# Two-layer encoder on one core: the second output product takes all its rows into the seven block products, and attention is drawn ahead

## The chip, the cores and the metric

The kernel runs on one core of one Trainium2 chip. The metric is device microseconds of one execution: the median before is 959.88 us of three runs (959.16 to 960.65).

## The reference

Two layers over 512 tokens of width 1024, in float32. What matters here is the second one (i = 1): eight query heads over two key/value heads, four memory heads, a gate, one output projection and the residual.

```python
for i in range(DEPTH):
    h = rmsnorm(x, norm_g[i])
    ...
    proj = jnp.einsum('bsd,de->bse', h, w_in_b[j])     # q | k | v | q_mem | gate
    o_mix = mixer_axial_gqa(...)                       # 8 heads of 128, rms norm, rotary, softmax
    ...
    o_mem = memory_attention(q_mem, mem_h, w_mem_kv[i], mem_qn_g[i], mem_kn_g[i])   # 4 heads
    y = jnp.concatenate([o_mix, o_mem], axis=-1) * jax.nn.silu(gate)                # 512 x 1536
    x = x + jnp.einsum('bse,ed->bsd', y, w_out[i])                                  # 1536 x 1024
```

## The kernel before

**Block products.** A 512-token projection is done by `s_chunk` (L376): the activations and the weights are cut into 2 x 2 blocks, and seven products of sums of blocks replace eight block products. The list `PRODUCTS` names the form of the activations that each takes: 12, 11, S1, S2, S4, S3, 22. S1 = A21 - A22, S2 = S1 - A11, S4 = A12 + S2, S3 = A11 - A21. Each product accumulates in PSUM banks (`pj`); at its end `keep` copies a bank to SBUF (ScalarE, a tile `sn`, L384) or `add` adds it to a kept one (VectorE, L401), and `diff` (L395) makes one difference of two kept tiles. What comes out goes to an evacuation `ev`.

**Precision.** Every float32 operand is split in a high part in the matmul's format and a low part, so each product is three matmuls: high by high (L172), low by high or high by low (L173), and the third (L176). For the weights the high part `wh` is a cast on ScalarE (L307) and the low part `wo` a subtraction on VectorE (L317), each for a 128 x 1024 tile. A *unit* is what one such tile feeds: in the output product 12 matmuls of 512 columns, in a gate 24 of 256.

**Weights.** `Weights` loads tiles on SyncE's queue, makes the sums T1 to T4 that the block products need by accumulating DMAs on GpSimd's queue, and casts two units ahead. `PLAN` lists the chunks in order, and for each kind how many tiles it has. The second layer's last entries are "W2b" (the block part of the output product, two units for each of the seven products) and twice "O1" (the rest).

**Order.** All engines' instructions are written in one program. A `Driver` counts slots, one for each unit on TensorE, and between units it advances generators by one step each: *urgent* ones (evacuations, forms) and *bulk* ones (attention), two steps of bulk a slot. `half()` advances the first bulk generator once more in the middle of a unit; the table `HALF` says every how many units this happens, for the gate chunks "m", "a", "b" and for the output product "o". Each engine executes its instructions in program order.

**Attention of the second layer.** `attn_b` (L1435) is a pipeline over 32 items, each a head and one of four blocks of 128 tokens. Per item: the score on TensorE (`sb`, three matmuls of 512 columns, L166 to L168), its maximum on VectorE (`nmb`, L1447), the exponential on ScalarE, the reciprocal (`rdb`, L1454), a scaling, four transposes on TensorE (`ptb`, L1467), the high part of them on ScalarE (`pbT`, L1471) and the low part on VectorE (`pbT`, L1476). After every second item comes the product with the values (`ob`): eight early matmuls, which need the high parts, and four late ones (L176), which need the low parts. The result is copied to `o` (L1494) and, except for heads 6 and 7, written to DRAM (`odb`).

**Gates.** `gates` (L794) makes three gate chunks of 512 columns: for the memory heads ("m"), heads 0 to 3 ("a") and heads 4 to 7 ("b"). Each evacuated 128 x 512 tile becomes SiLU (tanh on ScalarE, L838 on VectorE) and is multiplied by the head outputs, read back from DRAM as `og` (L828), or, for heads 6 and 7, from the tile in SBUF. The first two chunks stay as `yf`; of these 1024 rows `prep_y` makes the seven forms (`y`, `yS`; L875, L895, L900, L905), as `big` tiles. The third chunk is split in high and low parts as it is (L855), in `ys`.

**Output product.** `out_proj` (L913) loads the residual (`acc<-x1d`), runs `s_chunk` over the seven forms, adds each of its eight results to the residual by an accumulating DMA on GpSimd's queue, and `out_rest` (L763) does eight direct units for the 512 rows of heads 4 to 7, adds them on VectorE (L766) and stores the output from ScalarE's queue.

## Time and profile before

| | |
|---|---|
| median of three runs | 959.88 us |
| profiled execution | 960.29 us, of which the span is 958.4 us |
| granted TensorE clock | 1.00 |
| TensorE busy | 944.6 us (99%) |
| VectorE busy | 791.7 us (83%) |
| ScalarE busy | 678.0 us (71%) |
| GpSimd busy | 332.7 us (35%) |

The second layer's gates run from about 780 us, the output product from about 880 us. In a row of the timeline stand the start, the duration, the engine, the line, the operation, output and inputs, and in brackets the idle time before it and what ended it. Durations overlap on TensorE, where matmuls are pipelined, so the distance of two starts tells more than the duration of one.

### The profile page before, as it was taken

How to read it: one execution, taken by the hardware profiler on the slowest of the kernel's cores; microseconds unless marked ns; L12 is line 12 of the kernel's file. 1: busy time of each engine (PE TensorE's matmuls, PEld its weight loads, DVE VectorE, ACT ScalarE, POOL GpSimd, SP SyncE). 2: the span in 40 equal slices, each digit the busy share in tenths (PEclk: the TensorE clock that was granted, in tenths of full speed). 3: DMA queues.
4: the chain of work that ended last, by engine and by line, in shares of the span. 5: the costliest groups of instructions: out<-in, count | busy, mean ns of one | idle time of the engine just before them, and what ended most of it. 6: DMA issues, size and time to landing. Idle time of an engine off the chain costs nothing.

```text
span 958.4 us, 16597 instructions
## 1 busy us (share of the span) xinstructions
PE 944.6 (99%) x5682; PEld 831.9 (87%) x5682; DVE 791.7 (83%) x1415; ACT 678.0 (71%) x1693; POOL 332.7 (35%) x478
## 2 busy tenths in 40 slices
PE   8999999999999999999999999999999999999998
PEld 4879888888888888888889997878999999998886
DVE  4999586888888888979788999977988898769893
ACT  5875689686868686767775766537778876879770
POOL 1412423557454546463726111113232330011110
PEclk9999999999999999999999999999999999999999
DMA  9989946868787969696877989889885687787824
GB/s 354 320 193 344 304 111 173 291 133 258 152 260 156 262 154 264 154 259 138 234 185 185 268 204 308 280 250 328 230 189 117 190 237 173 210 207 187 248 54 127
DMA packets 87897, 208.23 MB, mean 217 GB/s; under 512 B 25219, under 2 KB 35203, under 8 KB 87813
## 3 DMA queue, kind: packets, MB, share of 16 engines
q1 hardware_dynamic: 68660, 144.18, 44.1%
q0 software_dynamic: 17856, 60.83, 34.2%
q10 hardware_dynamic: 1296, 2.16, 0.6%
q8 instruction: 45, 0.74, 0.3%
q14 instruction: 40, 0.32, 0.1%
HBM read 156.48 MB, written 11.86 MB: 176 GB/s over the span
## 4 chain that ended last, share of the span: by engine, by line
PE 90%; DVE 4%; DMA 3%; ACT 2%; issue 1%; POOL 0%; DVEq 0%; ACTq 0%; POOLq 0%
PE pj L173 24%; PE pj L172 23%; PE pj L176 23%; PE qT L604 2%; PE pt L1244 2%; PE sa L1163 1%; PE oo L1265 1%; PE sa L1159 1%; PE ptb L1467 1%; DMA og<-odb 1%; DVE wo L317 1%; PE xT L501 1%; PE ob L176 1%; PE row L625 1%; PE pmt L734 1%
## 5 line engine op out<-in xcount | busy, mean ns | idle before, releaser
L317 DVE TENSOR_TENSOR wo<-wl,wh 128x1024 fp32r<-128x1024 f32 x255 | 316.0, 1245 | 5.6 <-ACT wh L307 5.5
L307 ACT CAST wh<-wl 128x1024 fp32r<-128x1024 f32 x255 | 268.5, 1059 | 34.5 <-PE pj L173 16.9
L172 PE MATMUL pj<-wh,hS 128*128 128x512 f32 (+1 forms) x448 | 157.4, 365 | 1.6 <-ACT hS L567 1.6
L173 PE MATMUL pj<-wh,hS 128*128 128x512 f32 (+1 forms) x448 | 152.0, 353 | 0.0
L172 PE MATMUL pj<-wh,h 128*128 128x512 f32 (+1 forms) x336 | 117.9, 364 | 0.0
L173 PE MATMUL pj<-wh,h 128*128 128x512 f32 (+1 forms) x336 | 114.0, 353 | 0.0
L449 POOL TENSOR_TENSOR rstd<-mse,half 128x4 f32<-128x4 f32 (+2 forms) x96 | 100.5, 1046 | 8.0
L176 PE MATMUL pj<-wo,hS 128*128 128x512 f32 (+1 forms) x448 | 100.0, 352 | 0.2 <-DVE wo L317 0.2
L172 PEld LDWEIGHTS pj<-wh,hS 128*128 128x128 f32 x448 | 84.8, 189 | 12.1 <-ACT wh L307 1.8
L173 PEld LDWEIGHTS pj<-wh,hS 128*128 128x128 f32 x448 | 84.9, 190 | 10.2
L384 ACT COPY sn<-pj 128x512 f32<-128x512 f32 x132 | 73.2, 590 | 25.9 <-PE pj L176 23.7
L176 PEld LDWEIGHTS pj<-wo,hS 128*128 128x128 f32 x448 | 74.6, 189 | 12.4 <-DVE wo L317 0.6
L448 POOL TENSOR_SCALAR mse<-hss 128x4 f32<-128x4 f32 (+1 forms) x86 | 42.4, 493 | 123.0 <-ACT junk L592 118.6
L592 ACT ACTIVATE junk<-sn 128x128 f32<-128x128 f32 x264 | 79.1, 308 | 4.8 <-DVE sn L395 4.7
L1107 POOL TENSOR_TENSOR ta<-sn,tabs 128x128 f32<-128x128 f32 (+1 forms) x64 | 36.6, 579 | 119.5 <-DVE sn L597 92.4
L401 DVE TENSOR_TENSOR sn<-pj,sn 128x512 f32<-128x512 f32 x99 | 67.3, 683 | 9.2 <-PE pj L176 6.5
L176 PE MATMUL pj<-wo,h 128*128 128x512 f32 (+1 forms) x336 | 74.8, 352 | 0.0
L173 PEld LDWEIGHTS pj<-wh,h 128*128 128x128 f32 x336 | 63.7, 190 | 7.5
L172 PEld LDWEIGHTS pj<-wh,h 128*128 128x128 f32 x336 | 63.7, 189 | 7.5 <-DVE sn L401 0.2
L291 POOL DMA_DIRECT2D wl<-wl x33 | 29.1, 881 | 116.0 <-DVE wo L317 67.8
L176 PEld LDWEIGHTS pj<-wo,h 128*128 128x128 f32 x336 | 56.0, 189 | 8.8
L597 DVE TENSOR_TENSOR sn<-sn,rstd 128x512 f32<-128x512 f32 (+1 forms) x82 | 47.8, 592 | 7.9 <-POOL rstd L449 7.9
(240 smaller groups left out, 2328.6 us busy)
## 6 DMA issues: line engine op xcount, KB each, us to landing
wl<-in_wall_dram SPq DMA_DIRECT2D x222, 512.0 KB, 7.4
wl<-wl POOLq DMA_DIRECT2D x66, 512.0 KB, 5.6
wl<-in_wall_dram POOLq DMA_DIRECT2D x42, 512.0 KB, 8.4
acc<-sn POOLq DMA_DIRECT2D x16, 256.0 KB, 5.7
od<-o SPq DMA_DIRECT2D x11, 256.0 KB, 5.7
og<-od SPq DMA_DIRECT2D x10, 256.0 KB, 7.6
odb<-o SPq DMA_DIRECT2D x10, 256.0 KB, 3.2
og<-odb SPq DMA_DIRECT2D x10, 256.0 KB, 4.7
```

The source lines that it names most:

```text
L172: T.matmul(o, a, b, start=start, stop=False, skip_group_check=True)
L173: T.matmul(o, c, d, start=False, stop=False, skip_group_check=True)
L176: T.matmul(o, a, b, start=False, stop=stop, skip_group_check=True)
L307: A.copy(wh, self.tile[self.items[i]])
L317: V.tensor_tensor(wo, self.tile[key], wh.bitcast(F32), ALU.subtract)
L384: A.copy(t, b)
L401: V.tensor_tensor(t, b, t, ALU.subtract if q == "12" else ALU.add)
L448: G.tensor_scalar(e, ss, EPS, None, ALU.add)
L449: G.tensor_tensor(r, e, half[:, 0:n], ALU.pow)
L592: A.activation(jk, p[:, j * 128:(j + 1) * 128], AF.Square, scale=QS, accum_out=ss[:, j:j + 1])
L597: V.tensor_tensor(xn[:, 0:n], p.rearrange("p (a b) -> p a b", a=4)[:, 0:n], r[:, 0:n, None].to_broadcast([128, n, 128]), ALU.mult)
L1107: G.tensor_tensor(ta[:, 0:n], xn[:, 0:n, 0:32], ropeA[:, 0, b, s0:s0 + n], ALU.mult)
```

## The change

Only the second layer changes; TensorE's order is the same up to the second attention.

1. `PLAN`'s last three entries become "W3b", and `MERGED = False, True`: in the second layer all 1536 rows go through the seven products, three units each, 21 units. The first two units of each product take the forms of the first eight heads' rows as before (memory heads and heads 0 to 3), the third (x = 2) the forms of heads 4 to 7. `groups` sets the units' order: the third units of the first two products come a little later than their turn. The very last unit is split by PSUM bank.
2. `prep_l` makes the seven forms of heads 4 to 7 (`yl`, high part on ScalarE, low part on VectorE, L953) one by one. `Pace` holds each back until the unit given in `at_`.
3. `keep` adds a bank to a tile of the residual (`xb`, loaded with 256 KB each on SyncE's queue, paced) instead of copying it, so the accumulating DMAs of the result, `out_rest` and the direct splits of the third gate go; T4 of these weights is summed from DRAM.
4. `HALF` becomes 2 for all three gates and the output product.
5. `attn_b` takes heads 6 and 7 by halves of the tokens: both heads' blocks 0 and 1, then both heads' blocks 2 and 3, and `o_here` is kept by head and half.

```diff
-..., HALF, SET_B = 2, 2, 15, 1, 12, 1, 4, 1, {"a": 3, "b": 3, "o": 0}, 9
+..., HALF, SET_B = 2, 2, 15, 1, 12, 1, 4, 1, {"m": 2, "a": 2, "b": 2, "o": 2}, 9
...
-PLAN = [... + ["W2b"] + ["O1"] * 2
+PLAN = [... + ["W3b"]
...
+MERGED = False, True
...
+    def groups(units, merged=False):
+        if merged:
+            return [(0, 0), (0, 1), (1, 0), (0, 2), (1, 1), (1, 2)] + [(i, x) for i in range(2, 7) for x in range(3)]
+        return [(i, x) for i in range(7) for x in range(units)]
...
+                elif PLAN[c] in OUT:
+                    if not self.ripe(self.lo_at, (c, "T2", x), force, 1):
+                        continue
+                    self.tile[key] = self.tile[c, "T2", x]
+                    G.dma_start(self.tile[key], wall[d], accum_op=ALU.add)
...
         def keep(name, u, b):
-            t = snap[name, u] = s2(name="sn")
-            A.copy(t, b)
+            if base:
+                t = snap[name, u] = base({"z": "11", "s5": "22", "s2": "12", "s3": "21"}[name], u)
+                if name == "s3":
+                    c = snap[u, "22"] = snap["s5", u]
+                    V.tensor_tensor(c, c, b, ALU.subtract)
+                if name == "s2":
+                    V.tensor_tensor(t, t, b, ALU.subtract)
+                else:
+                    V.tensor_tensor(t, b, t, ALU.add)
+            else:
+                t = snap[name, u] = s2(name="sn")
+                A.copy(t, b)
...
+            for part in ((0,), (1,)) if (i, x) == (6, 2) else ((0, 1),):
...
+        def prep_l(at_):
...
+            def put(k, src):
+                t = m4(F32R, "yl")
+                A.copy(t[:, 0:512], src)
+                yield 1
+                V.tensor_tensor(t[:, 512:1024], src, t[:, 0:512].bitcast(F32), ALU.subtract)
+                YL[k] = t.rearrange("p (a k t) -> p a k t", a=2, k=2)
...
+            yield from wait((2, 0, 1))
+            yield from put("12", a12)
+            yield from at_(1)
+            yield from wait((2, 0, 0))
+            yield from put("11", a11)
+            yield from wait((2, 1, 0), (2, 1, 1))
+            yield from at_(3)
+            s1 = s2(name="ls")
+            V.tensor_tensor(s1, a21, a22, ALU.subtract)
+            yield 1
+            yield from put("S1", s1)
+            yield from at_(7)
...             # S2, at_(10) S4, at_(13) S3, at_(16) 22
...
     def attn_b():
+        item = [divmod(i, 4) for i in range(24)] + [(h, b + r) for r in (0, 2) for h in (6, 7) for b in range(2)]
...
-    out_proj(YW, ys, x1d, ev_o2, acc_b, HALF.get("o"))
+    out_merged(YW, YL, pace, load_b, lambda q, u: rest[q, u], ev_o2, HALF.get("o"))
```

Line numbers of the changed kernel differ: in it L173, L174 and L177 are the three matmuls, L335 the low part of weights, L1563 the transposes, L1572 the low part of probabilities, L423 and L429 the evacuation's `diff` and `add`.

On TensorE, in the first two units of the output product (`y` with its number is form 12 of the first eight heads' rows), there stands before:

```order
L176 MATMUL ob<-pbT,vb 128x256 x4
L1467 MATMUL ptb<-ident,pb 128x128 x4
L172 MATMUL pj<-wh,y_10896 128x512
L173 MATMUL pj<-wh,y_10896 128x512
L172 MATMUL pj<-wh,y_10896 128x512
```

And after:

```order
L177 MATMUL ob<-pbT,vb 128x256 x4
L1563 MATMUL ptb<-ident,pb 128x128 x4
L173 MATMUL pj<-wh,y_10805 128x512
L174 MATMUL pj<-wh,y_10805 128x512
L177 MATMUL pj<-wo,y_10805 128x512 x4
L1563 MATMUL ptb<-ident,pb 128x128 x4
L173 MATMUL pj<-wh,y_10805 128x512
```

Before, a whole unit of 12 matmuls and a score follow the transposes. Now only the second half of a unit (six matmuls) does, then the transposes of the next item; a whole unit, the early half of `ob` and its late half follow. These are items 28 and 29, the second token halves of head 6; the last product with the values comes behind the third unit of the output product, where before it comes behind the eleventh.

On VectorE at the same place, from one low part of probabilities (L1476) to the next, before (`ys` are sums for the forms, `yf` gated rows):

```order
L1476 TENSOR_TENSOR pbT<-ptb,pbT 128x4x128
L317 TENSOR_TENSOR wo<-wl,wh 128x1024
L895 TENSOR_TENSOR ys<-ys,yf 128x512 x2
L1447 TENSOR_REDUCE nmb<-sb 128x1
L1454 RECIPROCAL rdb<-denb 128x1
L1476 TENSOR_TENSOR pbT<-ptb,pbT 128x4x128
```

And after, between the low parts of items 28 and 29:

```order
L1572 TENSOR_TENSOR pbT<-ptb,pbT 128x4x128
L423 TENSOR_TENSOR sn<-sn 128x512
L429 TENSOR_TENSOR sn<-pj,sn 128x512
L335 TENSOR_TENSOR wo<-wl,wh 128x1024
L927 TENSOR_TENSOR ys<-ys,yf 128x512 x2
L869 SCALAR_TENSOR_TENSOR sn<-th,sn 128x512
L863 TENSOR_TENSOR yf<-sn,o 128x256 x2
L1550 RECIPROCAL rdb<-denb 128x1
L1572 TENSOR_TENSOR pbT<-ptb,pbT 128x4x128
```

The third gate's last results (`sn`, L423 and L429) and their SiLU and products (L869, L863) now stand between two low parts, where before there were a low part of weights, two sums and a maximum.

On VectorE further on, in front of the low part of form S1 of heads 4 to 7 (`yl`, the last row; numbers are those of the buffers), after:

```order
L967 TENSOR_TENSOR ls_11457<-yf_10676,yf_10677 128x512
L335 TENSOR_TENSOR wo_11448<-wl_10973,wh_11447 128x1024
L937 TENSOR_TENSOR yf_9590<-yf_9590 128x512
L937 TENSOR_TENSOR yf_9591<-yf_9591 128x512
L429 TENSOR_TENSOR xb_11287<-pj_11357,xb_11287 128x512
L335 TENSOR_TENSOR wo_11473<-wl_11029,wh_11472 128x1024
L907 TENSOR_TENSOR yS3_11503<-yf_9590,yS3_11503 128x512
L907 TENSOR_TENSOR yS3_11503<-yf_9591,yS3_11503 128x512
L953 TENSOR_TENSOR yl_11479<-ls_11457,yl_11479 128x512
```

Before, where S3 of the first eight heads is made:

```order
L317 TENSOR_TENSOR wo<-wl,wh 128x1024
L905 TENSOR_TENSOR yf<-yf 128x512 x2
L855 TENSOR_TENSOR y<-sn,y 128x2x256 x2
L1447 TENSOR_REDUCE nmb<-sb 128x1
L1454 RECIPROCAL rdb<-denb 128x1
L1476 TENSOR_TENSOR pbT<-ptb,pbT 128x4x128
L317 TENSOR_TENSOR wo<-wl,wh 128x1024
L875 TENSOR_TENSOR yS_11455<-yf,yS_11455 128x512 x2
```

The sums for S3 (L937) and its low parts (L907) stood among the attention; now the attention is over there, and an evacuation (L429, added to `xb`) and the difference for S1 of the last heads (L967) with its low part stand among them instead.

More of the change, by code (lines that the diff above doesn't have):

```diff
@@ L400, in add @@
                 diff(u)
-            V.tensor_tensor(t, b, t, ALU.subtract if q == "12" else ALU.add)
+            V.tensor_tensor(t, b, t, ALU.subtract if q == "12" and not base else ALU.add)
             yield 1
@@ L424, in s_chunk @@
                             drv.half()
-                    st = fresh and kk == 0 and (units == 2 or b == 0)
+                    st = fresh and not x and kk == 0 and (units == 2 or b == 0)
                     if tokens:
@@ L429, in s_chunk @@
                         mm_early(o, wh[:, k, bs], ah[:, kk], wh[:, k, bs], al[:, kk], st)
[L430 removed]
+                for b, k, kk, bs, o in regions(part):
                     if tokens:
[L432 removed]
+                        mm_late(o, ah[:, kk, bs], wo[:, k], kk == end)
                     else:
[L434 to L442 removed]
+                        mm_late(o, wo[:, k, bs], ah[:, kk], kk == end)
+            drv.free()
+            W.advance()
+            if x == last:
+                f, *arg = after[i]
+                for u in range(units):
+                    d = 2 if f is keep or tight and i == 1 else 2 + u + (units == 1 and i == 6 and not soon)
+                    drv.release(f(*arg, u, bank[s][u]), d)
+            drv.tick()
     def rstd_of(ss, n):
@@ L844, in ev @@
                         load()
[L845 removed]
+                    if not all((h, i) in o_here for h in hs):
                         yield 1
[L847 removed]
+                if not yt:
                     times(yf[g][j][:, i * 512:(i + 1) * 512])
@@ L934, in out_proj, with out_merged @@
         out_rest(ys, acc, done, evac)
+    def out_merged(YW, YL, pace, load, base, ev, half=False):
+        pace.start()
+        drv.spawn(load())
+        s_chunk(512, YW, ev, half=half, more=YL, base=base)
     xv = x.rearrange("(p c) d -> c p d", c=4)
@@ L1056, in put_od @@
         if i in DIRECT:
-            o_here[i] = t
+            for r in range(2):
+                o_here[i, r] = t
             return
```

165 lines of the change are left out of this document (98 added, 67 removed).

## The prediction

> **What bounds the kernel now.** I read the page first, then the windows of the last 180 us, then PE's waits, then the chain around each of them, and last the timeline of VectorE (DVE) in front of each wait.
>
> ```profile
> span 958.4 us, 16597 instructions
> PE 944.6 (99%) x5682; PEld 831.9 (87%) x5682; DVE 791.7 (83%) x1415; ACT 678.0 (71%) x1693; POOL 332.7 (35%) x478
> PE 90%; DVE 4%; DMA 3%; ACT 2%; issue 1%; POOL 0%; DVEq 0%; ACTq 0%; POOLq 0%
> ```
>
> TensorE is busy for nearly all of the span and carries nine tenths of the chain that ended last. So a matmul less is its whole time less, unless another engine then comes too late. Which engine that could be is read by stretches: the end of the queries with the first gate (780 to 800), the output product's block part with the last attention (880 to 925), and its end. The columns are the length, the busy time of PE, PEld, DVE, ACT and POOL, the granted clock, the DMA share and GB/s.
>
> ```profile
> 780.00:800.00 20.00, 20.00 (x160) 19.34 (x159) 19.93 (x36) 16.26 (x37) 6.06 (x7) 1.00 0.69 157
> ...
> 880.00:900.00 20.00, 20.00 (x114) 17.28 (x113) 18.90 (x31) 15.32 (x30) 1.73 (x2) 1.00 0.79 195
> 900.00:925.00 25.00, 24.42 (x135) 20.75 (x134) 21.31 (x33) 20.21 (x39) 2.92 (x4) 1.00 0.53 169
> 925.00:958.40 33.40, 29.63 (x131) 24.22 (x129) 15.42 (x23) 6.11 (x9) 4.05 (x5) 1.00 0.41 106
> ```
>
> The clock is full everywhere. VectorE is the second engine: 19.93 of 20 us at the first gate, 18.90 of 20 in the block product, and only in the last 33 us, where the direct sums run, is it half free. The change shortens TensorE's work exactly there and makes the forms of the last heads, which are VectorE work, earlier. PE's only waits in the second layer's last 250 us are two, both for the low part of transposed probabilities (pbT), which VectorE makes:
>
> ```profile
> PE ob L176 <- DVE pbT L1476: 1.3, 2, 0.7
> ```
> ```profile
> 870.54 0.74 PE L176 MATMUL ob<-pbT,vb 128*128 128x256 f32 x4 [0.68 <-DVE pbT L1476]
> 908.26 0.74 PE L176 MATMUL ob<-pbT,vb 128*128 128x256 f32 x4 [0.58 <-DVE pbT L1476]
> ```
>
> The chain shows what stood in front of VectorE in the first of them, and the timeline the second:
>
> ```profile
> 855.42 5.55 DMA odb<-o
> ...
> 860.99 4.39 DMA og<-odb
> ...
> 869.89 0.60 DVE pbT L1476
> 870.50 0.04 issue
> 870.54 0.74 PE ob L176 x4
> ```
> ```profile
> 902.66 0.69 DVE L828 TENSOR_TENSOR sn<-sn,og 128x512 f32<-128x512 f32 x1 [3.08 <-DMA og<-odb]
> 903.27 0.68 DVE L1447 TENSOR_REDUCE nmb<-sb 128x1 f32<-128x512 f32 x1
> 903.88 0.15 DVE L1454 RECIPROCAL rdb<-denb 128x1 f32<-128x1 f32 x1
> 903.95 0.67 DVE L1476 TENSOR_TENSOR pbT<-ptb,pbT 128x512 fp32r<-128x512 f32 x1
> 904.53 1.21 DVE L317 TENSOR_TENSOR wo<-wl,wh 128x1024 fp32r<-128x1024 f32 x1
> 905.67 1.28 DVE L875 TENSOR_TENSOR yS<-yf,yS 128x512 fp32r<-128x512 f32 x2
> ```
>
> Both begin with a head output that goes out to DRAM and back (5.55 and 4.39 us) and is multiplied at the head of VectorE's queue; in the second, VectorE stands idle for 3.08 us and works off its queue afterwards. The starts also give VectorE's prices, from start to start: 0.60 us for 512 columns (902.66 to 903.27, 0.61), 0.07 for a reciprocal, 1.14 for a low part of weights (wo, 904.53 to 905.67).
>
> **The change part by part.** *Fewer matmuls.* Of the 22 units of the output product 21 stay, since 1536 rows in seven products of three units replace 14 units and 8 direct sums. One unit is 12 matmuls:
>
> ```profile
> 927.27 0.39 PE L172 MATMUL pj<-wh,y 128*128 128x512 f32 x1
> ...
> 929.99 0.39 PE L172 MATMUL pj<-wh,y 128*128 128x512 f32 x1
> ```
>
> 929.99 - 927.27 = 2.72 us (0.227 a matmul): **-2.72 us**, all on the path.
>
> *The two waits.* With more half steps in the gates, the attention runs ahead: its last product stands behind the third unit of the output product, and before behind the eleventh. The head outputs of the third gate are then written and read earlier, and at both places the order now has other steps. One multiply with a read output (L859) still stands ahead of the low parts of items 27 and 28, but nothing of the wait of 3.08 us has to follow it there. I take both waits as gone: **-1.26 us** (bounds -1.26 and 0).
>
> *A new wait at the last heads.* The second order piece of the change shows what now lies between the low parts of items 28 and 29: 512-column steps L423, L429, L927 (two) and L869 at 0.60, one wo at 1.14, two 256-column products, a reciprocal and the low part itself. The rest of the prices:
>
> ```profile
> 791.53 0.42 DVE L1402 TENSOR_TENSOR sn<-ta,sb 128x256 f32<-128x256 f32 x1
> 791.86 0.42 DVE L1403 TENSOR_TENSOR sn<-ta,sb 128x256 f32<-128x256 f32 x1
> ```
> ```profile
> 893.50 0.60 PE L1467 MATMUL ptb<-ident,pb 128*128 128x128 f32 x4
> 893.86 0.48 PE L172 MATMUL pj<-wh,yS 128*128 128x512 f32 x1
> 894.17 0.40 PE L173 MATMUL pj<-wh,yS 128*128 128x512 f32 x1
> ```
> ```profile
> 894.76 0.69 DVE L1476 TENSOR_TENSOR pbT<-ptb,pbT 128x512 fp32r<-128x512 f32 x1 [0.29 <-ACT pbT L1471]
> ```
>
> A 256-column step is 0.33. Transposes hold PE for 0.36, the first matmul behind them takes 0.31 instead of 0.23, and the low part starts 1.26 after the transposes did. Counted from the transposes of item 28: its low part is done at 1.26 + 0.60 = 1.86, that of item 29 at 1.86 + 5 x 0.60 + 1.14 + 2 x 0.33 + 0.07 + 0.60 = 7.33, and PE sees it 0.05 later (869.89 + 0.60 against 870.54 in the chain), at 7.38. PE by then has done 0.36, six matmuls (1.36), the transposes of item 29 (0.36), one unit (2.72), the eight early matmuls of ob (256 columns, half of 0.227 each: 0.91) and twice the 0.08, together 5.87. It waits **+1.5 us** (bounds 0, if VectorE reaches item 28 with sums already done, and 2.3, if each of the steps runs at the top of its spread and the wo waits for its cast).
>
> *The first form of the last heads that has a sum of its own.* From the low part of 29 to that of yl S1 VectorE has six wo (6.84), 22 steps of 512 (13.20) and two of 256 (0.66): 20.7 us, and before item 31 it must wait about 0.6, since those transposes start 2.3 us after the low part of 29 and their low part can start 1.26 later, at 3.56, where VectorE is ready at 2.94. So 21.3, and 0.05 to PE. PE in that time has the late half of ob (0.45), two transposes (0.72), one unit (2.72) in two halves, the extra 0.16, another ob (1.36), five units (13.60) and the first matmul of yl S1 (0.23), together with the 0.05 at the start 19.3 us. The second matmul takes the low part: **+2.0 us** (bounds 0 and 3, in the same way). Behind it VectorE has 7.6 us of work per three units, 8.16 on PE, and the other forms come in time.
>
> *More half steps in the gates.* The three gates hold 10 half steps, and held 4. Each leaves 3.39 us from the start of a transpose to the late half of the ob that needs its low part (0.36 + half a unit 1.36 + three scores 0.68 + 0.91 + 0.08), where a whole unit leaves 4.75. The low part needs 1.86 plus what VectorE is late. The four of before show no wait, though VectorE is at 19.93 of 20 there: **0** (bounds 0 and 3.5, the second rival).
>
> *Keeps and sums.* The products are added by VectorE to a residual tile instead of being copied by ACT. Eight of VectorE's direct adds (L766) go and eight adds of this sort come, and their source is PSUM:
>
> ```profile
> L401 DVE TENSOR_TENSOR sn<-pj,sn 128x512 f32<-128x512 f32 x8 | 5.4, 682 | 0.0
> L900 DVE TENSOR_TENSOR yf<-yf,ys 128x512 f32<-128x512 f32 x2 | 1.3, 684 | 0.0
> ```
>
> Reading PSUM costs nothing here, 682 ns against 684, so they stand at 0.60 in the sums above. [...]
>
> ACT loses eight copies, and gains three casts of weights and the high parts of seven forms; with 15.32 of 20 us and then 6.11 of 33.4 it has room. The casts stand two units ahead of their use, and a cast queued behind an output transfer's issue has those two units, 5.4 us. POOL loses eight accumulating transfers and gains four sums of weights at 4.05 busy of 33.4; SP's eight residual loads of 256 KB take the place of four of 512 KB. All of that is hidden, **0** (bounds 0 and 0.5, at the end):
>
> ```profile
> 954.67 0.69 DVE L766 TENSOR_TENSOR acc<-pj,acc 128x512 f32<-128x512 f32 x1 [2.03 <-PE pj L176]
> ```
> ```profile
> out_dram<-acc ACTq DMA_DIRECT2D x8, 256.0 KB, 2.0
> ```
>
> The end is an add and a 256 KB transfer, as before; only the last two transfers are now issued 1.36 us apart and not 2.72, so their 2.0 us overlap.
>
> The sum: -2.72 - 1.26 + 1.5 + 2.0 = **-0.5 us**. The profiled execution took 960.29 us (1.9 around its span of 958.4), so 959.8 on its scale; it stands 0.41 above the median of 959.88, so 959.4.
>
> **The rivals.** *VectorE keeps up.* Neither new wait appears, as the two are differences of 1.5 and 2 us between chains of 7 and 21: a tenth less on VectorE closes the second, a fifth the first. For it: VectorE's average in 900 to 925 is 21.31 of 25, and attention pulled ahead moves its steps out of this stretch. Against: forms and adds come in, and the runs of the timeline are gapless. -2.72 - 1.26 = -3.98: 956.3 on the profile's scale, **955.9**.
>
> *The half steps cost more than the unit saves: slower.* At the first gate VectorE runs late already:
>
> ```profile
> 789.87 0.39 PE L168 MATMUL sb<-kbT,qb 128*128 128x512 f32 x1
> ```
> ```profile
> 792.80 0.68 DVE L1447 TENSOR_REDUCE nmb<-sb 128x1 f32<-128x512 f32 x1
> ```
>
> The maximum of a score that ends at 790.1 starts at 792.80, 2.7 us later. If a low part inherits that, it is done 1.86 + 2.7 = 4.56 after its transposes, 1.17 beyond the 3.39 that a half step leaves. Half of the six added ones would wait, as each wait lets VectorE catch up: 3 x 1.17 = 3.5 on top of -0.5, 963.3 by the profile, **962.9**. It decides where VectorE is more than 3.39 - 1.86 = 1.5 us late. For it: 19.93 of 20. [...] Against: an attention step brings PE some 1.8 us and VectorE 1.27 (a maximum, a reciprocal and a low part), so more of them per unit relieves VectorE.
>
> *The change doesn't do what it says* has no room: the order shows 12 matmuls fewer, and the first attention product that moves.
>
> **How the numbers follow.** Forecast (both new waits, about their size) 0.48, within 958.0 to 961.5; VectorE keeps up 0.32; half steps that wait 0.20. The range reaches down to the first rival, 955.7, and up to where the slower one begins to hold, 962.3; outside lies some 0.17 of the latter case and the far ends. Faster by over 0.2% (under 957.96) is the first rival and a tenth of the forecast, 0.42; slower (over 961.80) the second and 0.02, 0.22; 0.36 lies between. 0.2%, 1.9 us, is about what a measurement of this kernel can tell from no change.
>
> **What would show it.** Right: 12 matmuls fewer, no PE wait near the third gate's og, one PE wait of about 1.5 us at the ob of the last heads' first halves and one of about 2 at the first yl S1 unit, both with VectorE named and VectorE gapless in front. Wrong: neither wait (then nearly 4 us are gained), waits of about a microsecond at half steps in the gates (then it is slower), or a wait for wh, wo or a form of the first eight heads, which the sum holds at nothing.

## The result, and the profile after

The changed kernel took **964.32 us** (median of seven runs, 963.25 to 965.7) beside 960.65 for the kernel before on the same chip: ratio 1.0038, 95% interval 1.0026 to 1.0051, 3.67 us slower. The profiled execution took 963.25 us. Its page opens with the span, the engines' busy time, and, further down, the chain that ended last by engine:

```profile
span 961.5 us, 16603 instructions
PE 942.7 (98%) x5670; PEld 828.7 (86%) x5670; DVE 800.1 (83%) x1425; ACT 681.1 (71%) x1691; POOL 330.0 (34%) x474
...
PE 82%; DVE 9%; ACT 5%; DMA 2%; issue 1%; POOL 0%; SPq 0%; DVEq 0%; ACTq 0%; POOLq 0%
```

The 12 matmuls are gone (5670 against 5682). TensorE's share of the chain fell from 90% to 82%: VectorE and ScalarE now hold 14% of it, against 6% before. The windows tell where (length, then busy time of PE, PEld, DVE, ACT and POOL):

```profile
780.00:800.00 20.00, 18.24 (x132) 16.16 (x132) 17.14 (x32) 16.60 (x40) 5.79 (x7) 1.00 0.58 121
...
880.00:900.00 20.00, 18.80 (x126) 16.90 (x124) 16.90 (x31) 16.58 (x33) 2.60 (x3) 1.00 0.95 255
900.00:925.00 25.00, 22.88 (x110) 18.76 (x111) 24.18 (x35) 15.67 (x25) 3.25 (x4) 1.00 0.96 274
```

At the first gate TensorE lost 1.8 of 20 us, where before it lost none, and VectorE is *less* busy there than before (17.14 against 19.93). From 900 to 925 VectorE has no room left. TensorE's waits from 766 us to the end (line, what it waited for; total, times, longest):

```profile
PE pj L174 <- DVE yl L953: 1.7, 1, 1.7
PE ob L177 <- DVE pbT L1572: 1.6, 1, 1.6
PE ptb L1563 <- ACT pb L1547: 1.0, 2, 0.8
PE ob L173 <- ACT pbT L1567: 0.6, 1, 0.6
PE ob L173 <- ACT pb L1547: 0.4, 1, 0.4
PE qT L1460 <- DVE pbT L1572: 0.3, 1, 0.3
PE ob L173 <- DVE pbT L1572: 0.2, 1, 0.2
PE sb L167 <- ACT pb L1547: 0.2, 1, 0.2
```

The first two are the waits that the prediction gave 2.0 and 1.5. The other six rows were not in it: apart from the 0.6 (at 868 us, in the third gate) they all lie in the first gate, which runs here from 770 to 809 us (the first gate of before begins at 771, not at 780). Four of them, with their neighbours, on TensorE's timeline, and the two predicted ones at the end:

```profile
784.41 0.39 PE L169 MATMUL sb<-kbT,qb 128*128 128x512 f32 x1
785.02 0.66 PE L1563 MATMUL ptb<-ident,pb 128*128 128x128 f32 x4 [0.22 <-ACT pb L1547]
...
787.40 0.66 PE L1460 MATMUL qT<-ident,sn 128*128 128x128 f32 x4 [0.30 <-DVE pbT L1572]
788.24 0.50 PE L167 MATMUL sb<-kbT,qb 128*128 128x512 f32 x1 [0.17 <-ACT pb L1547]
...
791.96 0.66 PE L1563 MATMUL ptb<-ident,pb 128*128 128x128 f32 x4 [0.83 <-ACT pb L1547]
...
900.38 0.74 PE L177 MATMUL ob<-pbT,vb 128*128 128x256 f32 x4 [1.57 <-DVE pbT L1572]
...
922.09 0.50 PE L174 MATMUL pj<-wh,yl 128*128 128x512 f32 x1 [1.65 <-DVE yl L953]
```

The first two rows show that a wait costs more than its bracket: the starts are 0.61 apart, a 512-column matmul takes 0.23 from start to start, and 0.22 is listed as waiting, so 0.16 comes on top. At the other waits on this list it is 0.15 to 0.17 as well, but for 0.32 at 788.24. Four of the six waits name L1547, ScalarE's exponential. The transposes read the probabilities only after ScalarE has scaled them (L1554), so this is not their input. ScalarE's timeline around the wait of 0.83:

```profile
786.80 0.72 ACT L1554 ACTIVATE pb<-pb,rdb 128x512 f32<-128x512 f32 x1 [1.35 <-DVE rdb L1550]
...
790.51 0.72 ACT L1554 ACTIVATE pb<-pb,rdb 128x512 f32<-128x512 f32 x1
791.13 0.69 ACT L1547 ACTIVATE pb<-sb,nmb 128x512 f32<-128x512 f32 x1
791.70 0.21 ACT L1547 ACTIVATION_READ_ACCUMULATOR pb<-sb,nmb 128x1 f32 x1
```

The scaling was over at 791.23, the exponential at 791.91, and the transposes started at 791.96. What an exponential gives free is the score that it reads, in a PSUM bank, and the kernel lets scores, transposes and products with the values take turns on four banks (`at`, L153). The score at 788.24 reads no probabilities at all, and the transposes of queries (`qT`) at 787.40 read no `pbT`: they too can only have waited for a bank. That all six are waits for a bank is read from these rows and the kernel; no run changes the number of banks.

ScalarE itself had stood idle for 1.35 us, up to 786.80, for a reciprocal of VectorE. Why that was late is seen in VectorE's queue at that place:

```profile
783.40 0.42 DVE L1497 TENSOR_TENSOR sn<-ta,sb 128x256 f32<-128x256 f32 x1
783.74 0.42 DVE L1498 TENSOR_TENSOR sn<-ta,sb 128x256 f32<-128x256 f32 x1
784.08 0.69 DVE L628 TENSOR_TENSOR sn<-sn,rstd 128x512 f32<-128x512 f32 x1
784.80 0.69 DVE L1493 TENSOR_TENSOR ta<-sn,tabs 128x512 f32<-128x512 f32 x1
785.40 0.69 DVE L1494 TENSOR_TENSOR sb<-sn,tabs 128x512 f32<-128x512 f32 x1
786.01 0.68 DVE L1543 TENSOR_REDUCE nmb<-sb 128x1 f32<-128x512 f32 x1
...
788.22 0.16 DVE L1550 RECIPROCAL rdb<-denb 128x1 f32<-128x1 f32 x1 [0.27 <-ACT pb L1547]
788.69 0.69 DVE L1572 TENSOR_TENSOR pbT<-ptb,pbT 128x512 fp32r<-128x512 f32 x1 [0.31 <-ACT pbT L1567]
```

The norm and rotary steps of the last queries (L628, L1493, L1494, and the ends L1497 and L1498 of the ones before) stand ahead of the maximum of a score and the reciprocal behind it. From score to transposes an item goes through maximum (VectorE), exponential (ScalarE), reciprocal (VectorE), scaling (ScalarE); with half steps the next of these is due half a unit earlier, while VectorE's queue is as long as before. ScalarE, once late, has its other work ahead of the next exponential, and TensorE waits for the bank. VectorE then even stands idle twice for ScalarE (0.27 and 0.31): the round trip is late, while VectorE is not full. That is how VectorE can be less busy here and TensorE still wait.

### The profile page after: what moved, and what is told of

Its sections match the earlier page's. It is cut to its first block, busy times and chain, and to the rows that moved or that the text cites. A ratio compares the mean times of both kernels' runs of the same rounds, so it can differ in the third digit from the quotient of the medians.

```text
span 961.5 us, 16603 instructions
## 1 busy us (share of the span) xinstructions
PE 942.7 (98%) x5670; PEld 828.7 (86%) x5670; DVE 800.1 (83%) x1425; ACT 681.1 (71%) x1691; POOL 330.0 (34%) x474
## 4 chain that ended last, share of the span: by engine, by line
PE 82%; DVE 9%; ACT 5%; DMA 2%; issue 1%; POOL 0%; SPq 0%; DVEq 0%; ACTq 0%; POOLq 0%
PE pj L174 21%; PE pj L173 21%; PE pj L177 21%; DVE wo L335 2%; PE qT L635 2%; PE sa L1256 1%; PE oo L1358 1%; PE pt L1337 1%; PE sa L1252 1%; PE ptb L1563 1%; DMA wl<-in_wall_dram 1%; DMA acc<-in_x_dram 1%; ACT wh L325 1%; PE xT L532 1%; PE row L656 1%
## 5 line engine op out<-in xcount | busy, mean ns | idle before, releaser
L335 DVE TENSOR_TENSOR wo<-wl,wh 128x1024 fp32r<-128x1024 f32 x258 | 319.6, 1245 | 3.8 <-ACT wh L325 3.7
L325 ACT CAST wh<-wl 128x1024 fp32r<-128x1024 f32 x258 | 271.5, 1059 | 43.1 <-PE pj L174 26.1
L173 PE MATMUL pj<-wh,hS 128*128 128x512 f32 (+1 forms) x448 | 157.4, 365 | 1.7 <-ACT hS L598 1.7
L174 PE MATMUL pj<-wh,hS 128*128 128x512 f32 (+1 forms) x448 | 152.1, 353 | 0.0
L173 PE MATMUL pj<-wh,h 128*128 128x512 f32 (+1 forms) x336 | 117.9, 364 | 0.0
L174 PE MATMUL pj<-wh,h 128*128 128x512 f32 (+1 forms) x336 | 114.0, 353 | 0.0
L177 PE MATMUL pj<-wo,hS 128*128 128x512 f32 (+1 forms) x448 | 100.0, 353 | 0.2 <-DVE wo L335 0.2
L173 PEld LDWEIGHTS pj<-wh,hS 128*128 128x128 f32 x448 | 84.8, 189 | 12.2 <-ACT wh L325 1.8
L174 PEld LDWEIGHTS pj<-wh,hS 128*128 128x128 f32 x448 | 84.9, 190 | 10.3
L177 PEld LDWEIGHTS pj<-wo,hS 128*128 128x128 f32 x448 | 74.6, 189 | 12.4 <-DVE wo L335 0.6
L412 ACT COPY sn<-pj 128x512 f32<-128x512 f32 x124 | 68.7, 589 | 23.0 <-PE pj L177 22.2
L177 PE MATMUL pj<-wo,h 128*128 128x512 f32 (+1 forms) x336 | 74.9, 352 | 0.0
L429 DVE TENSOR_TENSOR sn<-pj,sn 128x512 f32<-128x512 f32 x93 | 63.4, 684 | 9.4 <-PE pj L177 6.4
L174 PEld LDWEIGHTS pj<-wh,h 128*128 128x128 f32 x336 | 63.7, 190 | 7.5
L173 PEld LDWEIGHTS pj<-wh,h 128*128 128x128 f32 x336 | 63.6, 189 | 7.5 <-DVE sn L429 0.2
L309 POOL DMA_DIRECT2D wl<-wl x31 | 27.4, 884 | 107.9 <-DVE wo L335 58.9
L177 PEld LDWEIGHTS pj<-wo,h 128*128 128x128 f32 x336 | 56.0, 189 | 8.8
L294 POOL DMA_DIRECT2D wl<-wl x34 | 32.2, 980 | 64.6 <-DVE wl L289 18.2
```

Source lines behind the costliest of these rows:

```text
L173: T.matmul(o, a, b, start=start, stop=False, skip_group_check=True)
L174: T.matmul(o, c, d, start=False, stop=False, skip_group_check=True)
L177: T.matmul(o, a, b, start=False, stop=stop, skip_group_check=True)
L294: G.dma_start(self.tile[key], self.tile[c, "T1", x], accum_op=ALU.add)
L325: A.copy(wh, self.tile[self.items[i]])
L335: V.tensor_tensor(wo, self.tile[key], wh.bitcast(F32), ALU.subtract)
```

## The experiments

The theory: the half steps at the first gate make TensorE wait there, as VectorE's queue still holds the queries' steps, and these waits are what the prediction lacks. The rival, told in each expectation for its run: the waits are only symptoms; with VectorE behind by some amount, what is taken from one wait comes back at the next. Ratios below are to the kernel before in the same session (959.8 to 960.7 us), with the 95% interval in brackets.

**The half steps out of the first gate, and half steps alone.** The change with fewer half steps, the kernel before with the change's table, and the kernel before with the reduced table:

```diff
# e1_half_a: the change; f5_before_half_a: the kernel before
-HALF = {"m": 2, "a": 2, "b": 2, "o": 2}      (before: {"a": 3, "b": 3, "o": 0})
+HALF = {"m": 0, "a": 1, "b": 2, "o": 2}
# e2_before_half: the kernel before
-HALF = {"a": 3, "b": 3, "o": 0}
+HALF = {"m": 2, "a": 2, "b": 2, "o": 2}
```

> The changed kernel with the three half steps of the first gate moved into the second gate (none in m, one in every unit of a, b and o as they are): the attention ends at the same unit of the output product. Theory A, the half steps of the first gate come where VectorE is still full with the queries, so TensorE's waits between 784 and 808 us (0.22, 0.30, 0.17, 0.24, 0.83, 0.39, together 2.15, some 3.3 with the 0.16 to 0.2 that each start costs) are their price: they vanish, 964.3 - 3.3 = 961.0. Theory B, the time is lost to VectorE in the output product alone, and half steps cost about the same wherever they stand: 964 to 965. The waits at the last heads (1.57) and at yl S1 (1.65) stay by both.

> The kernel before with the new table of half steps alone (2 in m, a, b and o), nothing merged. Theory A: the first gate's waits appear here too (+3.3), the two old waits for the low parts go (0.68 and 0.58, 1.6 with the starts): 960.6 + 1.7 = 962.3. Theory B: no wait of over 0.3 at the first gate, 960.6 - 1.6 = 959.0.

> The kernel before with the table of half steps of the fastest version so far (none in m, one in every unit of a, 2 in b and o), nothing merged. That version took 957.7 against 960.7. If its gain is the merged product's 12 matmuls and the table only removes the old waits, this comes out near the kernel before: 957.7 + 2.7 = 960.4. If the table alone gives the gain, 958.

Without half steps in "m" the change took 962.75 us, 1.0022 (1.0011 to 1.0032), and no wait is left from 766 to 890 us. The theory's 961.0 was missed by 1.8 us: the wait at the last heads grew, and two new ones of 0.40 and 0.53 stand behind it. On TensorE's timeline:

```profile
896.78 0.74 PE L177 MATMUL ob<-pbT,vb 128*128 128x256 f32 x4 [2.24 <-DVE pbT L1572]
```

It is 2.24 where it was 1.57. The kernel before with the change's half steps took 963.53, 1.0031 (1.0019 to 1.0042): as slow as the change, with no other part of it. Two of its waits:

```profile
792.86 0.66 PE L1467 MATMUL ptb<-ident,pb 128*128 128x128 f32 x4 [0.82 <-ACT pb L1451]
...
900.44 0.74 PE L176 MATMUL ob<-pbT,vb 128*128 128x256 f32 x4 [0.78 <-DVE pbT L1476]
```

The six waits of the first gate stand there with the same sizes within 0.01 us (0.83 there, 0.82 here). So the theory holds for the first gate, and the table of half steps alone costs about 3 us (0.0031 of 960). The kernel before with the reduced table took 960.18, 0.9995 (0.9986 to 1.0005): that table is harmless.

**The queries' steps moved away instead.** `YB` spaces the steps of the second layer's queries; here the rotary steps of heads 4 to 7's queries come three slots later, in the change and in the kernel before with the new half steps:

```diff
-YB = {..., 1: (1, 2, 1)}
+YB = {..., 1: (4, 2, 1)}
```

> The changed kernel with the rotary steps of the second half of the queries (heads 4 to 7, not needed before item 16) three slots later, so that four rounds of three 512-column steps on VectorE move from the first gate's begin (some 765 to 792 us) to its end. If the first gate's waits are VectorE's queue of query work, they go although the half steps stay: 963.7 - 3.3 = 960.4, and the output product's two waits stay at 1.57 and 1.65. Rival, the half step itself is too short for the chain maximum, exponential, reciprocal, scaling: the waits for ScalarE's pb stay, 963.7.

> The kernel before with the new table of half steps and the queries' rotary steps later, nothing merged. With the table alone it took 1.0031 of the kernel before (963.5 against 960.1). If those 3.4 us were VectorE's queue in the first gate, they go: 960.1 to 960.4. Against the run with the same two edits on the changed kernel it gives the worth of the merged product.

The change so took 962.3, 1.0026 (1.0017 to 1.0034), where the theory had 960.4. The first gate's waits are gone but for one, which now stands behind the moved steps:

```profile
805.37 0.39 PE L173 MATMUL ob<-pbT,vb 128*128 128x256 f32 x1 [1.00 <-DVE pbT L1572]
```

That confirms whose steps were in the way, and it is the rival on a small scale. The kernel before, with the new half steps and the later queries, took 962.03, 1.0021 (1.001 to 1.0031), with waits of 1.01, 0.57 and 0.78, 1.1 us more than the two of before; its span from the first score on is 1.95 longer. The rest lies in gaps under 0.25 us each and is left open.

**The forms of the last heads.** The wait for yl S1 was to go by making the form in one step, or by making other forms later, S2 and those behind it of the first eight heads:

```diff
# e3_yl_now: difference, cast and low part with no step of others between
-            yield 1
-            yield from put("S1", s1)
+            yield from put("S1", s1, True)
# e4_s2_late and f1_defer: after put("S1", s1), ahead of S2, S4, S3 and 22
-            yield 1
+            yield 2        (f1_defer: yield 5)
```

> The changed kernel with the form yl S1 made in one step (difference, high part, low part) where its three steps lay two units apart: its low part moves ahead of two low parts of weights and five steps of 512 columns, 5.3 us of VectorE's queue, and VectorE waits some 0.7 for ScalarE's cast. Theory: the wait of 1.65 at the first yl S1 unit goes and nothing is late behind it: 964.3 - 1.8 = 962.5. Rival, VectorE is behind over the whole stretch, and the wait moves to the next low part (weights, S2): 964.

> The changed kernel with the sums and forms S2, S4, S3 and 22 of the first eight heads one unit later: two sums of 0.60 leave the stretch between the low parts of items 28 and 29, and two low parts leave the stretch ahead of yl S1, which takes the two sums instead. By the queue sum the wait at the last heads falls from 1.57 to about 0.4 and the one at yl S1 stays at 1.65: 964.3 - 1.2 = 963.1. Rival, the low part of 29 waits for something else than VectorE's queue (the transposes' cast): 964.3, with the wait at 1.5.

> The changed kernel with the forms S2, S4, S3 and 22 of the first eight heads four units later (the run with one unit took a wait of 1.57 down to 0.36 and gave 1.27, 0.48 and 0.31 back at the yl units behind). Open is whether VectorE has too much work in the whole output product or only too early. Order alone: counted from the low part of item 29, yl S1 comes at 18.9 us on VectorE (before, 21.3) against 19.3 on TensorE, S2 of the first eight heads and all forms behind stay in time, and the waits fall to about 0.4 at the last heads and 0.2 at yl 12: 963.7 - 2.9 = 960.8. Too much work in all: the waits move to later forms again, 963.

In one step: 964.24, 1.0037 (1.0023 to 1.005). The wait for yl S1 went, and its size came back at the next form, S2:

```profile
930.90 0.50 PE L174 MATMUL pj<-wh,yl 128*128 128x512 f32 x1 [1.72 <-DVE yl L954]
```

One unit later for S2: 963.71, 1.0037 (1.0026 to 1.0047); the wait at the last heads fell from 1.57 to 0.36, and three waits for `yl` forms (1.27, 0.48 and 0.31) stand where one of 1.65 stood. Four units later: 962.23, 1.0014 (1.0002 to 1.0027), with 0.37 at the last heads and one of 1.12 at S2. These forms were not made too late but too early: made ahead of need, they stood in front of the probabilities' low parts. Deferring them far enough brought some 2.3 us (1.0014 against 1.0038, within about 1.7 us by the two intervals).

**Other places for the half steps.** If the first gate is the wrong place, they can be put into the later gates, in the change and, to have a pair, in the kernel before:

```diff
-HALF = {"m": 2, "a": 2, "b": 2, "o": 2}      (before: {"a": 3, "b": 3, "o": 0})
+HALF = {"m": 0, "a": 1, "b": 1, "o": 2}      (before: {"m": 0, "a": 1, "b": 1, "o": 0})
```

> The changed kernel with no half step in the first gate and one in every unit of the second and third: the attention ends behind the first unit of the output product and not behind the third. The comparison is with 960.1 for the kernel before and 963.7 for the changed one. Theory A (half steps cost only where VectorE is full with the queries; the waits of the output product are a queue of VectorE that is too long for the units it lies beside): VectorE has 15 of 20 us in these two gates, so no waits there; between the last low part of the first halves and yl S1 VectorE has 24.9 us and TensorE 26.0, so both waits of the output product go: 960.1 - 2.7 - 1.6 = 955.8. Rival, a unit with two attention items is too dense: a wait of 0.3 to 0.5 at most of the 14 units, 960 to 963.

> The kernel before with that same table of half steps (none in m, one in every unit of a and b), nothing merged. Theory A: the two waits of before (1.26, 1.6 with the starts) go and none comes: 960.1 - 1.6 = 958.5. Against the first kernel of this call it tells what the merged product alone is worth: 2.7 us, if VectorE's added work stays hidden. Rival as there: 960 to 963.

Both took the same again: 964.48, 1.0046 (1.0028 to 1.0064), and 964.32, 1.0046 (1.0029 to 1.0064). Both have new waits of 1.47 and 0.51 for the high part of probabilities at 864 and 871 us; half a unit is now too short for ScalarE in the third gate, where its casts, copies and the tanh stand ahead of the probabilities. The change has 2.48 as well, at its fourth unit, for the very first form of the last heads (12), and 0.99 at their S2. My expectation of 955.8 missed by 8.7 us.

**Work taken off VectorE.** Six of the eight kept banks copied by ScalarE and the residual added by GpSimd's accumulating DMAs, with the change's half steps (e6) and with those of e5 (e7); and ten sums of the forms computed on GpSimd instead (e9):

```diff
# e6_act_keep, e7_ab_keep (the two "s3" banks stay as they are)
-                t = snap[name, u] = base({...}[name], u)
-                ...
-                    V.tensor_tensor(t, b, t, ALU.add)
+                t = snap[name, u] = s2(name="sn")
+                A.copy(t, b)
+                if name == "s5": base("22", u, t)      # x1d added by DMA
# e9_pool_sums
-            V.tensor_tensor(s1, a21, a22, ALU.subtract)
+            G.tensor_tensor(s1, a21, a22, ALU.subtract)      # and S2, S4, S3, also of the first eight heads
```

> The changed kernel, with six of its eight kept banks copied by ScalarE again, and the residual added to them by accumulating DMAs on GpSimd's queue: VectorE has two steps of 0.60 fewer ahead of the low part of yl S1 and two fewer ahead of S2. If VectorE's queue is what the wait at yl S1 is made of, it falls from 1.65 to about 0.45, and the one at the last heads stays at 1.57: 963.7 - 1.3 = 962.4. Rival, the copies and the accumulating DMAs bring a new wait (a cast of weights behind ScalarE's copies): 963.7 or more.

> The two edits together: half steps in every unit of the second and third gate, and six kept banks on ScalarE. By theory A the first alone leaves no wait in the output product, so this adds nothing: 955.8, within 0.5 of the first alone. If VectorE is still behind there, it is lower by up to 2.4, four steps of 0.60.

> The changed kernel with ten of the form sums (S2, S4, S3 of the first eight heads, two each; S1, S2, S4, S3 of the last heads) on GpSimd, which has little to do there. VectorE loses two steps of 0.60 between the low parts of items 28 and 29 and five ahead of yl S1. By the queue sums the wait at the last heads falls from 1.57 to 0.4, the one at yl S1 (1.65) goes: 963.7 - 3.0 = 960.7. Rival: a sum on GpSimd takes over 2 us, ScalarE's casts of the forms wait for it and the casts of weights behind them: 963.7 or more, with TensorE waiting for wh, wo or a form.

The copies by ScalarE gave 962.85, 1.0026 (1.0016 to 1.0036), as expected; the wait for yl S1 shrank to

```profile
921.44 0.50 PE L174 MATMUL pj<-wh,yl 128*128 128x512 f32 x1 [0.46 <-DVE yl L951]
```

while 1.57 at the last heads, which no kept bank precedes, stayed. On top of e5 the medians show nothing that can be told (964.36, 1.0038, 1.0022 to 1.0053): its 2.48 stayed; the place of that wait, at 909 us, lies ahead of most of the kept banks. The 0.99 at S2 went, but the profile lost 1.7 us to a fall of the clock (last section), so what the copies are worth there stays open. The sums on GpSimd made it much slower, 967.7, 1.008 (1.0067 to 1.0093), with 2.80 at the last heads; in its profile some 1.7 us of the loss are a fall of the clock behind this wait (last section). VectorE's and then GpSimd's timeline ahead of it:

```profile
891.41 1.79 DVE L859 TENSOR_TENSOR yf<-sn,og 128x512 f32<-128x512 f32 x1
...
893.79 0.67 DVE L1572 TENSOR_TENSOR pbT<-ptb,pbT 128x512 fp32r<-128x512 f32 x1
...
898.28 3.64 DVE L335 TENSOR_TENSOR wo<-wl,wh 128x1024 fp32r<-128x1024 f32 x1
```
```profile
890.97 3.38 POOL L927 TENSOR_TENSOR ys<-ys,yf 128x512 f32<-128x512 f32 x2 [0.47 <-DVE yS L907]
...
897.99 2.85 POOL L932 TENSOR_TENSOR yf<-yf,ys 128x512 f32<-128x512 f32 x2
```

A low part of weights that takes 1.2 us took 3.64. It started 0.29 us after two sums on GpSimd, ran past their end at 900.84 by about its own 1.1 us, as if it had got nowhere while they ran. Beside the two sums before it (890.97 to 894.35) a product of two tiles in SBUF took 1.79 us, where the median of this line is 0.69, while a low part of probabilities, which reads one operand from PSUM, was not held up (0.67). That GpSimd's sums held the first two up, and that the place of the operands decides, is read from these three rows; no run varies it.

**Together.** The later queries, GpSimd's sums and ScalarE's copies (e11); then, without GpSimd's sums, the deferred forms with ScalarE's copies and one of three ways out of the first gate: later queries (f2), the reduced half steps (f3), or half steps every third unit of "m" (f4); and f3 without the copies (f6):

```diff
# f2, f3, f4 and f6: yield 5 ahead of S2, S4, S3, 22; copies as in e6 (not in f6)
# f2_defer_q_late
+YB = {..., 1: (4, 2, 1)}
# f3_defer_half_a, f6_half_a_defer
+HALF = {"m": 0, "a": 1, "b": 2, "o": 2}
# f4_defer_half_m3a
+HALF = {"m": 3, "a": 1, "b": 2, "o": 2}
```

> Three edits together on the changed kernel: queries' rotary steps later, the form sums on GpSimd, six kept banks on ScalarE. If VectorE's queue is the whole cause, all waits over 0.6 go (5.4 with the starts) : 963.7 - 3.3 - 3.5 = 956.9, faster than the kernel before (960.1). If the sums on GpSimd cost as their rival says, 960 or more.

> The same, with six kept banks on ScalarE and the queries' rotary steps three slots later. If waits are only VectorE's queue in these two places: 962.3 (rotary steps later alone) - 2.9 = 959.4, with a wait of 1.0 left near 805 us and 0.6 near 867. If the merged product costs in another way, 961 or more.

> Forms four units later, six kept banks on ScalarE, and the half steps of the first gate moved into the second (that alone took 1.0022 of the kernel before, with waits of 2.24, 0.40, 0.53 and 1.67 behind 896 us). Order alone: 2.24 falls by the two sums to 1.0, 0.53 and 1.67 go, 0.40 (ScalarE's cast) stays: 962.1 - 3.6 = 958.5, faster than the kernel before at 959.9. Too much work in all: 961.

> As the kernel with half steps in the second gate, and with two half steps kept in the first gate (at its third and sixth unit), so that the attention ends behind the second unit of the output product. If a half step in the first gate costs by VectorE's lateness there, two of them cost at least 1 us of waits near 785: 959.5 to 960.5, slower than without them; if not, 958 or less.

> The fastest version so far without its ScalarE copies: the changed kernel, half steps of the first gate moved into the second, forms four units later, all eight banks kept on VectorE. In the run with that order alone (f1) a wait of 1.12 stood at yl S2, behind two kept banks that VectorE added (1.2). Theory: the same wait here, 957.7 + 1.3 = 959.0. If VectorE has room at yl S2 with this table, 957.7.

| | us | ratio (95%) | TensorE's waits after 766 us |
|---|---|---|---|
| e11 | 964.54 | 1.0043 (1.003 to 1.0056) | 1.01, 0.57, 0.17, 2.73, 0.72 |
| f2 | 959.73 | 0.9991 (0.9979 to 1.0004) | 1.00, 0.57, 0.36 |
| **f3** | **957.73** | **0.997 (0.9959 to 0.9982)** | 1.04 |
| f4 | 959.61 | 0.9988 (0.9976 to 1.0) | 0.46, 0.57, 0.99, 0.30 |
| f6 | 958.97 | 0.9984 (0.9973 to 0.9994) | 1.03, 0.16, 1.12 |

f3 beats both kernels. Its page, its windows at the two places, and its one wait:

```profile
span 955.2 us, 16616 instructions
PE 941.1 (99%) x5670; PEld 828.5 (87%) x5670; DVE 795.8 (83%) x1419; ACT 683.4 (72%) x1697; POOL 337.9 (35%) x480
```
```profile
780.00:800.00 20.00, 20.00 (x159) 19.20 (x157) 19.44 (x35) 16.28 (x34) 6.91 (x6) 1.00 0.70 154
...
900.00:925.00 25.00, 24.86 (x116) 20.58 (x115) 24.96 (x35) 17.69 (x24) 8.80 (x10) 1.00 0.96 222
```
```profile
894.79 0.74 PE L177 MATMUL ob<-pbT,vb 128*128 128x256 f32 x4 [1.04 <-DVE pbT L1570]
```

VectorE has 24.96 of 25 us from 900 to 925, more than in the change's 24.18, and no wait of TensorE is listed there: the same engine, as full, with its queue in another order and six kept banks off it. f4 takes back part of the gain with half steps at every third unit of the first gate. Only 0.46 of its waits stands in that gate; 0.57 and 0.99, both for the high part of probabilities, stand at 870 and 892 us, where the attention then runs further ahead.

What the merged product is worth is read from pairs with the same half steps and the same queries (e8 has none in the output product, but there the attention ends behind its first unit in both):

| pair | without merge | with merge | difference |
|---|---|---|---|
| half steps of the change (e2, the change) | 1.0031 | 1.0038 | none that can be told |
| half steps in the later gates (e8, e5) | 1.0046 | 1.0046 | none that can be told |
| later queries (e12, e10) | 1.0021 | 1.0026 | none that can be told |
| reduced half steps, forms deferred, copies on ScalarE (f5, f3) | 0.9995 | 0.997 | -0.0025, 2.4 us |

The last is, within some 1.4 us by the two intervals, the 2.72 us of 12 matmuls; there the two kernels wait about the same (0.35 and 0.93 in f5, 1.04 in f3). In the first three, new waits give it back: e2 has 0.78 at the last heads, and the change 1.57 there and 1.65 at yl S1; the pair with later queries is alike, and e5 has 2.48 and 0.99 where e8 has 0.73, 0.33 and 0.52.

## Why the prediction was wrong

*Fewer matmuls*, -2.72: right. 5670 matmuls are left, and the last pair agrees with their worth where both kernels wait about the same.

*The two waits of before*, -1.26: right. Neither stands in the profile after.

*A new wait at the last heads*, +1.5: measured 1.57. VectorE's queue between the two low parts was the one that I had summed; from 895.84 to 899.65 there is no gap in it:

```profile
895.84 1.22 DVE L335 TENSOR_TENSOR wo<-wl,wh 128x1024 fp32r<-128x1024 f32 x1
896.98 1.29 DVE L927 TENSOR_TENSOR ys<-ys,yf 128x512 f32<-128x512 f32 x2
898.18 0.69 DVE L869 SCALAR_TENSOR_TENSOR sn<-th,sn 128x512 f32<-128x512 f32 x1
...
899.65 0.67 DVE L1572 TENSOR_TENSOR pbT<-ptb,pbT 128x512 fp32r<-128x512 f32 x1
```

*The first yl form with a sum of its own*, +2.0: measured 1.65. *The end*, 0 within 0 to 0.5: the span ends 3.94 us after the start of the last add (957.56), before 3.73 (954.67), so about +0.2.

***More half steps in the gates*, 0: this step failed.** The argument was that the four half steps of before show no wait "though VectorE is at 19.93 of 20 there". They are not there. The table of before has no "m": its four stand in the second and third gate, after 800 us, and the 19.93 is the window of the first gate. I joined a table's entry and a window without seeing that they belong to different stages. The price itself was set against one wait alone, that of the late half of `ob` for the low part (3.39 us after the transposes). None of the six waits of the first gate is that one: they are at transposes, a score and early halves of `ob`, for PSUM banks that ScalarE's exponential or VectorE's low part gives free late. The prediction has no term for these. They are 2.15 us (0.22, 0.30, 0.17, 0.24, 0.83, 0.39), and with 0.16 for each 3.1; the one at 868 us, in the third gate, where the early half of `ob` waits for the high part from ScalarE, adds 0.56, or 0.7.

The second error was the sentence that more attention steps per unit relieve VectorE, as each brings TensorE more time than VectorE. That weighs sums of work. What decided was the order of VectorE's queue: attention drawn ahead meets the queries' steps, and e10 showed that it is those.

The sum, with 0.16 for each wait, old and new: -2.72 - 1.58 + 1.73 + 1.81 + 3.1 + 0.7 + 0.2 = +3.2. From the first score of the second attention on, where the two programs part, the profiles differ by 3.8 (961.5 - 773.47 against 958.4 - 774.20), the medians by 3.67; about 0.5 is left. An estimate for it: the instruction behind a wait is slow to follow as well. Four late matmuls of `ob` take 0.58 from 900.38 to the next start, and 0.48 undisturbed (799.55 to 800.03); behind the other waits of the first gate it is mostly 0.06 to 0.11 more, and there are seven waits more than before.

Of the rivals, the slower one came nearest, at 962.9: the right place, with 3.5 us the right size, and the right condition, VectorE 2.7 us late at the first gate. Its means was off, so that the size fits is in part luck. I let the *low part* inherit the lateness and the late half of `ob` wait for it, while of the 2.15 us 1.61 were waits for a bank that the exponential gives free, and the other 0.54 for one that a low part does. It had 0.20, and should have had more: 19.93 of 20 and the maximum 2.7 us late, both quoted, spoke for it, and against it stood the misplaced row and the weighing of sums. That "VectorE keeps up" is disproved by the two waits that came.

## What to carry to other kernels

When a step is to run denser, look at the queue of the engine that serves it *at that place*, with what else stands there; that a denser order is free in another stage says nothing. A late round trip doesn't show as a full engine: VectorE was at 17.14 of 20 where it made TensorE wait, and at 24.96 of 25 where it did not, so read what stands ahead of the awaited instruction, not the share. Work made early on a shared engine can cost as much as work made late; deferring forms to their need and leaving the dense stage alone, with six kept banks on ScalarE, turned 3.7 us lost into 2.9 gained (f3, 0.003 of 960). And where instructions of several kinds share PSUM banks, look also at who gives a bank free: the six waits of the first gate (2.15 us) are, as read here, for banks and not for operands.

## What the runs showed of the hardware

In the changed kernel's profile a wait cost TensorE about 0.16 us beyond the idle time that is listed for it (0.61 between two starts, where a matmul takes 0.23 and 0.22 is listed; 0.15 to 0.17 at the other waits from 784 us on, 0.32 at 788.24), and what followed the wait was mostly slower by 0.06 to 0.11 (0.58 instead of 0.48 for four late matmuls).

In e9 a VectorE operation with two SBUF operands, started beside GpSimd operations of the same kind, took 3.64 us for 1.2, while one with a PSUM operand beside two other such operations took 0.67, as usual. Two sums on GpSimd took 2.85 us there, and they are 0.60 each on VectorE.

In two profiles TensorE's granted clock fell to 0.50 behind a wait, of 2.48 us in e7 (up to 908.79) and of 2.80 in e9 (up to 904.04). For e7 the windows of one microsecond give it in the column behind POOL:

```profile
909.00:910.00 1.00, 1.00 (x5) 0.82 (x5) 0.97 (x3) 0.00 (x0) 0.00 (x0) 1.00 1.06 434
910.00:911.00 1.00, 1.00 (x4) 0.82 (x4) 0.96 (x3) 0.00 (x0) 0.00 (x0) 0.67 0.97 395
911.00:912.00 1.00, 1.00 (x4) 0.72 (x3) 1.00 (x2) 0.25 (x1) 0.45 (x1) 0.50 1.00 377
912.00:913.00 1.00, 1.00 (x4) 0.81 (x3) 1.00 (x2) 0.73 (x2) 0.53 (x2) 0.50 0.54 205
913.00:914.00 1.00, 1.00 (x4) 0.77 (x4) 1.00 (x3) 1.00 (x2) 0.76 (x1) 0.62 1.22 141
```

0.33 + 0.50 + 0.50 + 0.38 = 1.7 us are lost. In e9 the windows from 904 to 908 us have 0.66, 0.50, 0.50 and 0.64, again 1.7. It came in two of the four profiles with a wait over 2.4 us: in e5 (2.48) and e11 (2.73) the clock is 1.00 from 890 to 920. e7's runs with a mean clock of 1.00 took 962.0 to 963.1 us, the others 964.4 to 965.0 (e11's runs divide alike, e5's don't). What decides whether the clock falls behind such a wait is not shown by these runs.
